# Binary cross-entropy on 8192 x 8192: whole-chunk clips, negations and logarithms, and another order of the last loads and negations

## The chip, the cores and the metric

The kernel runs on one core of one Trainium2 chip. The metric is the device time of one execution in microseconds (us). "The time before" is the median of three executions; beside them one execution was recorded by the hardware profiler, and all rows of "the profile" and "the trace" come from that one.

The engines that this kernel uses are DVE (VectorE), ACT (ScalarE), POOL (GpSimd, here only as an issuer of DMAs) and SP (SyncE, an issuer of DMAs too). A DMA transfer is spread over 16 DMA engines; each engine moves 8 of the 128 rows of a transfer.

## The reference

```python
def reference(pred: np.ndarray, target: np.ndarray) -> np.ndarray:
    eps = 1e-7
    pred = np.clip(pred, eps, 1 - eps)
    return -(target * np.log(pred) + (1 - target) * np.log(1 - pred))
```

Both inputs and the output are 8192 x 8192 in fp32. The target holds only zeros and ones, so the value of an element is -log(|p + t - 1|), with p the clipped prediction.

## The kernel before

The 67 million elements are seen as 128 partitions times 524288 columns and cut into chunks, each of which is one contiguous stretch of DRAM with one row for each partition. There are 39 chunks: chunk 0 (the "first" one, 10240 columns), chunks 1 to 35 with `WIDE` = 14336 columns each, and three small ones from `TAIL` (5632, 5632 and 1024 columns; called a, b and c in this document). In the code z is 35, the last wide chunk, and n is 39.

Two buffers hold all data. `ring_p` has three slots of 14336 fp32 columns; chunk k lies in slot k mod 3, is loaded there, is computed in place, and is stored from there. The three small chunks share one slot, side by side. `ring_t` has a single slot of 14336 bf16 columns for the target, so a target can be loaded only when the chunk before has used its own. The DMA turns the target's fp32 into bf16 while it loads.

A chunk passes five instructions, all in place in `ring_p`:

- `clip` (L85, DVE): max with EPS and min with 1 - EPS.
- `merge`, first part (L91, DVE): (t - 1) + p. It is the last reader of `ring_t`.
- `merge`, second part (L94, ACT): the absolute value.
- `merge`, third part (L95, ACT): the logarithm.
- `negate` (L99, DVE): times -1.

Each is applied to the two halves of a chunk one after the other (`halves`), except for the small chunks, where it is applied to the whole.

The order of the work is written out by hand: `tc.manual_schedule()` keeps the instructions of each engine in the order of the program, and the framework adds the waits between engines. So an instruction that waits holds up all that stands behind it on its engine.

The queues: pred of chunk 0 is loaded on ACT's queue; all other loads (L70 for pred, L73 for target) are issued by GpSimd. Stores (L79) are issued by GpSimd as well up to chunk z - 1; from chunk z on they are issued by SP. On GpSimd the order in the loop is: target k + 1, store k, pred k + 2. In the last round of the loop (k = z - 1) pred of all three small chunks is issued; their targets come behind the merges of chunk z.

At the end DVE's order is: negation of the first half of z, clips of a, b and c, merge of a, negation of the second half of z (with the store of z behind it), merge of b, negation of a, merge of c, negation of b, negation of c.

Of the kernel before, what the change touches and what calls it, by code (L numbers as in the profile page):

```python
# [1 line left out]

# [4 lines left out]

EPS = 1e-7

WIDE = 14336  # L10
SLOTS = 3
TAIL = (5632, 5632, 1024)
ROWS = (108, 12, 8)


@with_exitstack
def kernel(
    ctx: ExitStack,
    tc: tile.TileContext,
    pred: bass.AP,  # L20
    target: bass.AP,
    out: bass.AP,
):
    nc = tc.nc
    fp32 = mybir.dt.float32
    low = mybir.dt.bfloat16
    Alu = mybir.AluOpType
    Act = mybir.ActivationFunctionType
    P = nc.NUM_PARTITIONS

    R, C = pred.shape
    total = R * C // P
    rest = total - sum(TAIL)
    n = rest // WIDE
    first = rest - n * WIDE
    assert 0 < first <= WIDE and n > 4 and sum(TAIL) <= WIDE
    spots = [(first, 0)]
    spots += [(WIDE, k % SLOTS * WIDE) for k in range(1, n + 1)]
    c = (n + 1) % SLOTS * WIDE
    for w in TAIL:  # L40
        spots.append((w, c))
        c += w
    n = len(spots)
    z = n - 1 - len(TAIL)
    starts = [sum(w for w, _ in spots[:k]) * P for k in range(n)]

    pool = ctx.enter_context(tc.tile_pool(name="rings", bufs=1))
    ring_p = pool.tile([P, SLOTS * WIDE], fp32, name="ring_p", tag="ring_p")
    ring_t = pool.tile([P, WIDE], low, name="ring_t", tag="ring_t")
    warm = pool.tile([1, 8], fp32, name="warm", tag="warm")  # L50

    def chunk(ap, k):
        flat = ap.rearrange("r c -> (r c)")
        w = spots[k][0]
        return flat[starts[k] : starts[k] + w * P].rearrange("(p w) -> p w", p=P)

    def cols(ring, k, part, c):
        w = spots[k][0]
        i, m = part
        return ring[:, c + i * w // m : c + (i + 1) * w // m]  # L60

    def p_of(k, part=(0, 1)):
        return cols(ring_p, k, part, spots[k][1])

    def t_of(k, part=(0, 1)):
        return cols(ring_t, k, part, spots[k][1] % WIDE)

    def load_p(k):
        queue = nc.scalar if k == 0 else nc.gpsimd
        queue.dma_start(out=p_of(k), in_=chunk(pred, k))  # L70

    def load_t(k):
        nc.gpsimd.dma_start(out=t_of(k), in_=chunk(target, k))  # L73

    def store(k):
        queue = nc.sync if k >= z else nc.gpsimd
        r = 0
        for rows in ROWS if k == n - 1 else (P,):
            queue.dma_start(out=chunk(out, k)[r : r + rows, :], in_=p_of(k)[r : r + rows, :])  # L79
            r += rows  # L80
        assert r == P

    def clip(k, *part):
        p = p_of(k, *part)
        nc.vector.tensor_scalar(  # L85
            out=p, in0=p, scalar1=EPS, scalar2=1 - EPS, op0=Alu.max, op1=Alu.min
        )

    def merge(k, *part):
        p, t = p_of(k, *part), t_of(k, *part)  # L90
        nc.vector.scalar_tensor_tensor(  # L91
            out=p, in0=t, scalar=1.0, in1=p, op0=Alu.subtract, op1=Alu.add
        )
        nc.scalar.activation(out=p, in_=p, func=Act.Abs)  # L94
        nc.scalar.activation(out=p, in_=p, func=Act.Ln)  # L95

    def negate(k, *part):
        p = p_of(k, *part)
        nc.vector.tensor_scalar(out=p, in0=p, scalar1=-1.0, scalar2=None, op0=Alu.mult)  # L99

    halves = (0, 2), (1, 2)
    tail = range(z + 1, n)
    with tc.manual_schedule():
        load_p(0)
        load_t(0)
        load_p(1)
        nc.vector.memset(warm, 1.0)  # L107
        nc.scalar.activation(out=warm, in_=warm, func=Act.Ln)  # L108
        for h in halves:
            clip(0, h)  # L110
        for k in range(z):
            for h in halves:
                merge(k, h)
            load_t(k + 1)
            for h in halves:
                negate(k, h)
            for h in halves:
                clip(k + 1, h)
            store(k)
            for j in (k + 2,) if k + 2 <= z else tail if k + 2 == z + 1 else ():  # L120
                load_p(j)
        for h in halves:
            merge(z, h)
        for j in tail:
            load_t(j)
        negate(z, halves[0])
        for j in tail:
            clip(j)
        merge(z + 1)
        negate(z, halves[1])  # L130
        store(z)
        merge(z + 2)
        negate(z + 1)
        store(z + 1)
        merge(z + 3)
        negate(z + 2)
        store(z + 2)
        negate(z + 3)
        store(z + 3)


# [1 line left out]
_INS = ['pred', 'target']  # L143
_OUTS = [((8192, 8192), 'float32')]


# [23 lines left out]
```

## Time and profile before

| | |
|---|---|
| median of three executions | 1877.36 us (1874.84 to 1878.22) |
| the profiled execution: its time | 1875.12 us |
| the profiled execution: its span | 1873.3 us |
| busy: DVE, ACT, POOL | 1118.1 (60%), 901.6 (48%), 282.8 us (15%) |
| read from HBM, written to HBM | 536.87 MB, 268.44 MB |
| wide target, issue to landing (median) | 35.2 us |
| wide pred load, issue to landing (median) | 44.4 us |
| wide store on GpSimd's queue, issue to landing (median) | 31.1 us |

The span runs from the first to the last instruction of the core; the time of the same execution is 1.8 us longer. A row of the timeline gives the start in the span, the duration, the engine, the line of the kernel, the operation, what is written and read with the shape, the number of instructions merged into the row, and in brackets how long the engine was idle before it and whose work ended that. A DMA instruction on POOL is a row of its own: its duration is the time that GpSimd took to issue it, not that of the transfer. The queue q0 (software_dynamic) is GpSimd's, q1 is SP's and q10 is ACT's.

### The profile page before, as it was taken

The page shows a single profiled execution, that of the slowest core. Times are in us where ns is not written, and L with a number is a line of the kernel's source. Part 1 is how long each engine was busy: PE and PEld are TensorE (multiplying, and loading weights), DVE is VectorE, ACT ScalarE, POOL GpSimd, SP SyncE. Part 2 cuts the span into 40 slices and gives each one's busy share as a digit, 9 for nine tenths or more (in the row PEclk, how much of TensorE's full clock was granted, in tenths as well). Part 3 has the DMA queues.
Part 4 walks back from the last instruction along what each step waited for, and adds up shares of the span by engine and source line. Part 5 has one row for each costly group of instructions (what it writes and reads, how often), then busy time and mean ns, then how long its engine had stood idle before and what let it go on. Part 6 is the DMA issues. An engine that isn't in the chain of part 4 may idle for free.

```text
span 1873.3 us, 697 instructions
## 1 busy us (share of the span) xinstructions
DVE 1118.1 (60%) x226; ACT 901.6 (48%) x152; POOL 282.8 (15%) x116
## 2 busy tenths in 40 slices
DVE  3666565555665566666555665556656655566565
ACT  2654444455555544444445555554444444555554
POOL 0111111111110111111111111011111111111010
DMA  9999999999999999999999999999999999999998
GB/s 334 347 358 356 353 354 351 353 355 356 363 374 372 373 370 354 362 358 353 353 355 354 359 364 374 372 372 370 359 359 356 354 354 354 354 362 362 373 359 315
DMA packets 16870, 671.14 MB, mean 358 GB/s; under 512 B 1889, under 2 KB 1889, under 8 KB 2273
## 3 DMA queue, kind: packets, MB, share of 16 engines
q0 software_dynamic: 16128, 652.22, 97.4%
q1 hardware_dynamic: 592, 13.63, 1.7%
q10 hardware_dynamic: 144, 5.24, 0.7%
q14 instruction: 6, 0.04, 0.0%
HBM read 536.87 MB, written 268.44 MB: 430 GB/s over the span
## 4 chain that ended last, share of the span: by engine, by line
DMA 67%; issue 28%; ACT 2%; DVE 2%; POOL 0%; POOLq 0%; DVEq 0%
DMA ring_t<-in_target_dram 65%; DMA ring_p<-in_pred_dram 1%; DVE ring_p L91 1%; ACT ring_p L95 1%; ACT ring_p L94 1%; DVE ring_p L99 0%; DVE ring_p L85 0%; POOL out_dram L79 0%; POOL ring_p L70 0%; DVEq L165 0%; POOLq L73 0%; POOLq L79 0%; DVEq L91 0%
## 5 line engine op out<-in xcount | busy, mean ns | idle before, releaser
L94 ACT ACTIVATE ring_p<-ring_p 128x7168 f32<-128x7168 f32 (+3 forms) x75 | 451.6, 6021 | 950.5 <-DVE ring_p L91 950.5
L91 DVE SCALAR_TENSOR_TENSOR ring_p<-ring_t,ring_p 128x7168 f32<-128x7168 bf16 (+3 forms) x75 | 554.8, 7437 | 237.0 <-DMA ring_t<-in_target_dram 237.0
L99 DVE TENSOR_SCALAR ring_p<-ring_p 128x7168 f32<-128x7168 f32 (+3 forms) x75 | 285.0, 3801 | 472.3 <-ACT ring_p L95 472.3
L95 ACT ACTIVATE ring_p<-ring_p 128x7168 f32<-128x7168 f32 (+3 forms) x75 | 452.1, 6029 | 2.4
L85 DVE TENSOR_SCALAR ring_p<-ring_p 128x7168 f32<-128x7168 f32 (+3 forms) x75 | 281.8, 3799 | 29.1 <-DMA ring_p<-in_pred_dram 29.1
L79 POOL DMA_DIRECT2D out_dram<-ring_p x35 | 126.9, 3625 | 713.7 <-DVE ring_p L99 713.7
L73 POOL DMA_DIRECT2D ring_t<-in_target_dram x39 | 20.7, 531 | 809.7 <-DVE ring_p L91 808.9
L70 POOL DMA_DIRECT2D ring_p<-in_pred_dram x38 | 135.3, 3561 | 0.0
L108 ACT ACT_TABLE_LOAD x1 | 1.3, 1283 | 1.1 <-PEq L154 1.1
L107 DVE MEMSET warm<- 1x8 f32 x1 | 0.1, 65 | 0.8 <-PEq L154 0.8
L108 ACT ACTIVATE warm<-warm 1x8 f32<-1x8 f32 x1 | 0.2, 207 | 0.0
L154 POOL MEMSET const-float32-0.0<- 128x1 f32 x1 | 0.1, 98 | 0.2 <-issue 0.2
L154 POOL MEMSET const-bfloat16-1.0<- 128x1 bf16 x1 | 0.1, 101 | 0.0
L154 POOL MEMSET const-float32-1.0<- 128x1 f32 x1 | 0.1, 98 | 0.0
L154 POOL MEMSET const-uint8-127<- 128x1 uint8 x1 | 0.1, 98 | 0.0
## 6 DMA issues: line engine op xcount, KB each, us to landing
ring_p<-in_pred_dram POOLq DMA_DIRECT2D x35, 7168.0 KB, 44.4
out_dram<-ring_p POOLq DMA_DIRECT2D x34, 7168.0 KB, 31.1
ring_t<-in_target_dram POOLq DMA_DIRECT2D x35, 3584.0 KB, 35.2
out_dram<-ring_p SPq DMA_DIRECT2D x1, 7168.0 KB, 18.4
ring_p<-in_pred_dram POOLq DMA_DIRECT2D x2, 2816.0 KB, 35.6
out_dram<-ring_p SPq DMA_DIRECT2D x2, 2816.0 KB, 14.7
ring_p<-in_pred_dram ACTq DMA_DIRECT2D x1, 5120.0 KB, 25.9
out_dram<-ring_p POOLq DMA_DIRECT2D x1, 5120.0 KB, 18.0
```

Source lines behind the costliest of these rows:

```text
L70: queue.dma_start(out=p_of(k), in_=chunk(pred, k))
L73: nc.gpsimd.dma_start(out=t_of(k), in_=chunk(target, k))
L79: queue.dma_start(out=chunk(out, k)[r : r + rows, :], in_=p_of(k)[r : r + rows, :])
L85: nc.vector.tensor_scalar(out=p, in0=p, scalar1=EPS, scalar2=1 - EPS, op0=Alu.max, op1=Alu.min)
L91: nc.vector.scalar_tensor_tensor(out=p, in0=t, scalar=1.0, in1=p, op0=Alu.subtract, op1=Alu.add)
L94: nc.scalar.activation(out=p, in_=p, func=Act.Abs)
L95: nc.scalar.activation(out=p, in_=p, func=Act.Ln)
L99: nc.vector.tensor_scalar(out=p, in0=p, scalar1=-1.0, scalar2=None, op0=Alu.mult)
L107: nc.vector.memset(warm, 1.0)
L108: nc.scalar.activation(out=warm, in_=warm, func=Act.Ln)
L154: nc = _bacc.Bacc("TRN2", target_bir_lowering=False, num_devices=1)
```

## The change

- The first chunk has 8192 columns and the small ones have 6656, 6656 and 1024.
- The clip of every wide chunk and of the first one is one instruction instead of two.
- The logarithm leaves `merge` and gets a function of its own, `log`. In the loop, for every k but 1, the two halves get DVE's merge and the absolute value, then one logarithm and one negation follow for the whole chunk. For k = 1 and for z both stay in halves.
- In the loop's last round no pred of a small chunk is loaded. Behind the merges of z the loads are issued chunk by chunk: pred a, target a, pred b, target b, pred c, target c.
- At the end DVE's order becomes: negation of the first half of z, clip a, negation of the second half of z (store of z behind it), merge a, clip b, merge b, negation a, clip c, merge c, negation b, negation c.

```diff
-TAIL = (5632, 5632, 1024)
+TAIL = (6656, 6656, 1024)
...
         nc.scalar.activation(out=p, in_=p, func=Act.Abs)
+
+    def log(k, *part):
+        p = p_of(k, *part)
         nc.scalar.activation(out=p, in_=p, func=Act.Ln)
...
-        for h in halves:
-            clip(0, h)
+        clip(0)
         for k in range(z):
             for h in halves:
                 merge(k, h)
+                if k == 1:
+                    log(k, h)
             load_t(k + 1)
-            for h in halves:
-                negate(k, h)
-            for h in halves:
-                clip(k + 1, h)
+            if k == 1:
+                for h in halves:
+                    negate(k, h)
+            else:
+                log(k)
+                negate(k)
+            clip(k + 1)
             store(k)
-            for j in (k + 2,) if k + 2 <= z else tail if k + 2 == z + 1 else ():
-                load_p(j)
+            if k + 2 <= z:
+                load_p(k + 2)
         for h in halves:
             merge(z, h)
-        for j in tail:
+            log(z, h)
+        a, b, c = range(z + 1, n)
+        for j in a, b, c:
+            load_p(j)
             load_t(j)
         negate(z, halves[0])
-        for j in tail:
-            clip(j)
-        merge(z + 1)
+        clip(a)
         negate(z, halves[1])
         store(z)
-        merge(z + 2)
-        negate(z + 1)
-        store(z + 1)
-        merge(z + 3)
-        negate(z + 2)
-        store(z + 2)
-        negate(z + 3)
-        store(z + 3)
+        merge(a)
+        log(a)
+        clip(b)
+        merge(b)
+        log(b)
+        negate(a)
+        store(a)
+        clip(c)
+        merge(c)
+        log(c)
+        negate(b)
+        store(b)
+        negate(c)
+        store(c)
```

More of the change, by code (lines that the diff above doesn't have):

```diff
@@ L101 @@
     halves = (0, 2), (1, 2)
-    tail = range(z + 1, n)
     with tc.manual_schedule():
```

## The prediction

> **What bounds the kernel now.** I read the page first, then the chain of waits, the timeline of one middle chunk, the timelines and windows of the first 110 us and of the last 80 us, and last the packet records behind the DMA rows.
>
> ```profile
> DVE 1118.1 (60%) x226; ACT 901.6 (48%) x152; POOL 282.8 (15%) x116
> ...
> DMA  9999999999999999999999999999999999999998
> ...
> q0 software_dynamic: 16128, 652.22, 97.4%
> ```
>
> No compute engine is near full; the DMA engines are, from first slice to last. So fewer or wider instructions save nothing by themselves. The change can act only where it makes the DMA engines wait, or stop waiting. One middle chunk in the timeline (start, duration):
>
> ```profile
> 1079.43 15.16 DVE L91 SCALAR_TENSOR_TENSOR ring_p<-ring_t,ring_p 128x7168 f32<-128x7168 bf16 x2 [6.89 <-DMA ring_t<-in_target_dram]
> ...
> 1094.89 0.53 POOL L73 DMA_DIRECT2D ring_t<-in_target_dram  x1 [22.23 <-DVE ring_p L91]
> ...
> 1105.58 6.18 ACT L95 ACTIVATE ring_p<-ring_p 128x7168 f32<-128x7168 f32 x1
> 1111.79 3.89 DVE L99 TENSOR_SCALAR ring_p<-ring_p 128x7168 f32<-128x7168 f32 x1 [8.38 <-ACT ring_p L95]
> 1115.59 7.70 DVE L85 TENSOR_SCALAR ring_p<-ring_p 128x7168 f32<-128x7168 f32 x2
> 1115.97 3.63 POOL L79 DMA_DIRECT2D out_dram<-ring_p  x1 [20.56 <-DVE ring_p L99]
> 1119.59 3.82 POOL L70 DMA_DIRECT2D ring_p<-in_pred_dram  x1
> 1130.11 15.16 DVE L91 SCALAR_TENSOR_TENSOR ring_p<-ring_t,ring_p 128x7168 f32<-128x7168 bf16 x2 [6.82 <-DMA ring_t<-in_target_dram]
> ```
>
> Target lands at 1079.36, the next one at 1130.04: a period of 50.7 us, which is three wide transfers of 16.9 us (each DMA engine moves 8 of the 128 rows, 2.11 us a row in the packet records). The ring serves target, store, pred in turn. The store of this chunk is ready when L79 ends, at 1119.60; the target ahead of it keeps the last engine busy until 1129.7. So it comes 10 us early. L79 and L70 take 3.63 and 3.82 us where L73 takes 0.53: each was issued while a clip ran and ended 0.1 us after that clip half. GpSimd doesn't get a DMA out while DVE runs the clips; L73 at 1797.79, beside a merge, took 0.53.
>
> The end:
>
> ```profile
> 1828.04 6.02 DVE L91 SCALAR_TENSOR_TENSOR ring_p<-ring_t,ring_p 128x5632 f32<-128x5632 bf16 x1 [4.18 <-DMA ring_t<-in_target_dram]
> 1833.98 3.88 DVE L99 TENSOR_SCALAR ring_p<-ring_p 128x7168 f32<-128x7168 f32 x1
> ...
> 1837.89 23.13 SPq L79 DMA_DIRECT2D out_dram<-ring_p  x6
> ```
>
> ```profile
> 1832.00:1838.50 6.50, 6.50 (x3) 4.41 (x1) 0.00 (x0) 1.00 0.10 20
> 1839.00:1871.00 32.00, 12.72 (x5) 16.61 (x5) 0.00 (x0) 1.00 0.93 395
> ```
>
> The window's last columns are DMA share and GB/s. The last loads end at 1835.6 on the slowest engine, the wide chunk's store starts at 1838.8: 3.2 us of idle DMA, because its second negation stands behind the merge of the first small chunk. From there all stores run back to back to the end.
>
> **The change, part by part.** The sum goes against the profiled execution: span 1873.3, time 1875.12.
>
> *Middle chunks (k = 2 to 34).* From the groups by form: ACT 6.18 us for 7168 columns, 4.47 for 5120, so 0.834 ns a column and 12.15 for 14336. DVE tensor_scalar 3.89 and 2.83, so 0.52 ns a column and 7.60 whole. Merge and both Abs stay in halves; the second Abs starts when the second merge ends (1094.6), ends 1100.8; the whole logarithm ends 1112.97 (now 1111.76); the whole negation 1120.6 (now 1115.7); the whole clip 1128.1 (now 1123.3). L79 is issued at 1120.9, inside the clip, and I take it to be held to the clip's end plus 0.12: 1128.2, 48.9 us after the landing (now 40.2). L70 then goes out at once, 0.53. The clip is done 1.9 us before the next target lands, so no merge waits. The store is ready 8.6 us later, covered by the target transfer still in flight, as long as that lasts. When the ring had run empty in the start phase, L79 ended at 62.29 and its first packet ran at 62.85, 0.57 later, with rows at full speed. 1128.2 + 0.57 = 1128.8, against 1129.7 on the slowest DMA engine. Faster engines would wait some us, but they run up to 4.6 us ahead now and no landing depends on them. So the cover holds by 0.9 us: I cost the loop at 0. Bounds: below nothing no, since the slowest engine is already never idle; above, the row around 107 us, where a store's L79 ended 3.5 to 4 us before the target was through and the target's last row took 3.1 instead of 2.13: 0.95 a chunk, 33 chunks, 31 us. I take 0, because the row at 62 is the nearer (there L79 ended 0.4 us ahead on the slowest engine and the last row stayed 2.13), and keep both.
>
> The Trainium skill (DMA: Bandwidth & Descriptors, section Anatomy of one DMA) gives some 2.0 us of fixed time per DMA, setup and completion, where the rows here show 0.57 + 0.33 = 0.9. By the skill's figure two chunks would take an estimated 48.9 + 50.7 + 2.0, so 50.8 us each, and the loop 2 us more; no trace here shows 2.0.
>
> *Start.* 8192 columns for 10240 take 3 x 2048/14336 x 16.9 = 7.2 us of transfers from the front and put them into the small chunks. Pred and target of chunk 0 alternate row by row, 16 rows of 1.22 instead of 1.53, so pred lands at 22.1 (now 26.65); clip 4.4, to 26.5; merges to 35.2; L73 goes out at 35.5, before pred 1 is through (40), where now it comes as the ring runs dry (43.3; 1 to 1.5 us lost). Second Abs to 38.8, logarithm 7.0 to 45.9, negation to 50.3, then the whole clip of chunk 1 to 57.8 holds store 0: data from 58.5, while target 1 ended at 57.0: 1.5 us idle. Store 0 9.8 us, pred 2 16.9, target 2 17.0: lands at 102.8, now 111.4. 8.6 earlier, of which 7.2 is only moved: a gain of 1.4 (0.5 to 2.5). Logarithms and negations in halves for k = 1 keep store 1 ready at 101.7, in time.
>
> *Tail.* T0 is the landing of the last wide target, 1789.8 now. Small rows of 6656 columns take 0.985 us (5632: 0.833), 7.9 a transfer. After: store z-1 to T0+16.6, pred a to 24.5, target a to 32.4 (its issue waits for a half merge only, T0+8). ACT ends its two halves at T0+32.4 as now. DVE clips a to 28.5, negates the second half to 36.3: store z starts at T0+37.3 (SP's issue to data took 0.9), where now it starts at T0+49.0. That is what the move of the negation buys. But by then only pred a and target a are in, and pred b, target b, pred c and target c are still queued, where now nothing is. Two queues share an engine row by row:
>
> ```profile
> ring_p<-in_pred_dram ACTq DMA_DIRECT2D x1, 5120.0 KB, 25.9
> ...
> out_dram<-ring_p SPq DMA_DIRECT2D x1, 7168.0 KB, 18.4
> ```
>
> 5120 KB beside the other queue took longer than 7168 KB alone. So from T0+37.3 each load row of 0.985 waits for a store row of 2.12: pred b has 3 rows left, and ends at 46.6; target b has 5 of 8 rows in when store z is through (T0+62.1) and ends at 65.1; pred c and target c at 67.8. DVE's queue is in written order: the merge of b waits for target b, and behind it stands the negation of a, whose logarithm was done at T0+54.9. Merge b 65.5 to 72.5, negation a to 76.1, store a from 77.0 to 84.9. All else has been moved by 67.8: 9.2 us idle. Logarithm b ends 84.1, negation b 87.8, store b from 88.7: 3.8 us idle, to 96.6; store c to 97.9, and 2.7 us from there to the end, as now. T0+100.6, now T0+83.5.
>
> *Sum.* T0 comes 8.6 earlier, the tail is 17.1 longer: **+8.5**, span 1881.8, time 1883.6. The median of the runs before, 1877.36, lies 2.2 above the profiled execution; on it the forecast is 1877.4 + 8.5 = **1886**.
>
> **Rivals.**
> 1. *Loads are served first (faster).* If store z on SP's queue did not slow the loads on GpSimd's, target b would land at T0+48.4, merge b end at 55.5, store a be ready at 60, store b at 71.6, and all stores would run back to back behind store z, to T0+87.5: 87.5 - 83.5 - 8.6 = -4.6, 1873. It decides at target b landing before T0+56. For it: the two queues that shared rows at the start were ACT's and GpSimd's, not SP's. Against: 25.9 us for 5120 KB. Chance 0.12.
> 2. *The late store starves the ring in every chunk (much slower).* The 0.9 us cover is a sum of five durations; if the event at 107 us is the rule, 0.95 x 33 = 31 us more, 1917; a part of it, 1894 to 1905. Against: nothing of the kind at 62. Chance 0.25.
> 3. *Nothing to see.* If an engine took two load rows to each store row, the 11 load rows would be through at T0+59.8, merge b at 67.2, store a ready at 71.6, and 5.4 of the 9.2 us idle would not be: +3, 1880. For it, nothing; against, the start's rows alternated one for one. Chance 0.08.
> That instructions stay split in the changed kernel I leave out: each is one call.
>
> **How the numbers follow.** My case has 0.55, its own range 1881 to 1891 (start 0.5 to 2.5, tail 4 either way). A measurement of this kernel can tell about 0.2%, 3.8 us, from no change. Faster: rival 1's most, 0.10. Same: rival 3 and the rest of rival 1, 0.09. Slower: my case, rival 2, 0.81. The range leaves out half of rival 1 and the upper third of rival 2: 1873 to 1908.
>
> **What would show it.** Right: L79 in the loop near 7.3 us and L70 near 0.5; target landings still 50.7 apart; target 2 landing near 103; the small b target landing some 65 us after the last wide one; a window of nearly no DMA of about 9 us before store a and one of about 4 before store b. Wrong: landings 51 to 52 apart with a dip in DMA share at each store (rival 2); the b target within 50 us and no gap ahead of store a (rival 1); or L79 at 0.5 us inside the clip, which would refute the held issue.

## The result, and the profile after

The changed kernel takes 1896.7 us (median of five executions, 1893.4 to 1897.6) against 1878.2 for the kernel before (five executions). The ratio estimated from all of them is 1.0088, 95% interval 1.0071 to 1.0105. The forecast was slower, 1886 against 1877.4; the sign was right, the size about half of what came. The profiled execution has a span of 1895.7 us (1873.3 before), its time is 1897.6. The comparison of the steps below is between these two spans: +22.4 us.

The same lines of the page:

```profile
DVE 1110.3 (59%) x156; ACT 898.5 (47%) x118; POOL 298.2 (16%) x116
...
DMA  9999999999999999999999999999999999999996
...
q0 software_dynamic: 16128, 652.22, 96.9%
```

DVE has 70 instructions fewer and ACT 34, and together they are busy 11 us less. Nothing of that is seen in the time: the DMA engines are full as before, but for the last slice. One middle chunk in the timeline:

```profile
1076.62 15.16 DVE L91 SCALAR_TENSOR_TENSOR ring_p<-ring_t,ring_p 128x7168 f32<-128x7168 bf16 x2 [2.04 <-DMA ring_t<-in_target_dram]
...
1098.02 12.15 ACT L98 ACTIVATE ring_p<-ring_p 128x14336 f32<-128x14336 f32 x1
1110.20 7.63 DVE L102 TENSOR_SCALAR ring_p<-ring_p 128x14336 f32<-128x14336 f32 x1 [18.42 <-ACT ring_p L98]
1117.74 7.62 DVE L85 TENSOR_SCALAR ring_p<-ring_p 128x14336 f32<-128x14336 f32 x1
1118.12 7.36 POOL L79 DMA_DIRECT2D out_dram<-ring_p  x1 [25.52 <-DVE ring_p L102]
1125.47 0.53 POOL L70 DMA_DIRECT2D ring_p<-in_pred_dram  x1
1127.75 15.16 DVE L91 SCALAR_TENSOR_TENSOR ring_p<-ring_t,ring_p 128x7168 f32<-128x7168 bf16 x2 [2.39 <-DMA ring_t<-in_target_dram]
```

Each duration is the one worked out ahead (12.15, 7.60, 7.60, 7.3, 0.5) to 0.1 us, and the store's issue ends 48.9 us after the target's landing (1125.48 - 1076.6), as forecast. But the next merge starts 51.13 us after the last one, not 50.7. The end:

```profile
1860.57 7.09 DVE L91 SCALAR_TENSOR_TENSOR ring_p<-ring_t,ring_p 128x6656 f32<-128x6656 bf16 x1 [17.34 <-DMA ring_t<-in_target_dram]
1867.58 3.62 DVE L102 TENSOR_SCALAR ring_p<-ring_p 128x6656 f32<-128x6656 f32 x1
...
1871.22 15.05 SPq L79 DMA_DIRECT2D out_dram<-ring_p  x5
```

```profile
1829.63 56.65 SPq L79 DMA_DIRECT2D out_dram<-ring_p  x6
```

```profile
1842.00:1861.00 19.00, 1.66 (x2) 6.14 (x2) 0.00 (x0) 1.00 0.99 344
1862.00:1872.00 10.00, 9.96 (x4) 4.30 (x1) 0.00 (x0) 1.00 0.00 1
1872.50:1880.00 7.50, 1.30 (x2) 7.47 (x3) 0.00 (x0) 1.00 0.93 398
1880.00:1883.50 3.50, 3.49 (x2) 1.23 (x2) 0.00 (x0) 1.00 0.00 0
```

The single row is SP's: store z is issued at 1829.63, when pred b is half in and target b still to come. DVE waits 17.3 us for target b, and the negation of a, whose logarithm is done, stands behind that wait. DMA stands still for 10 us ahead of store a and for 3.5 ahead of store b. Ahead of these gaps, in the packet records, a row of target b (1.00 us) and a row of store z (2.13 us) follow each other in turn on each DMA engine, from 1838.4 to 1857.1.

Where the 22.4 us come from can be read from the starts of two merges, of chunk 2 and of the last wide chunk, before and after:

```profile
111.49 15.16 DVE L91 SCALAR_TENSOR_TENSOR ring_p<-ring_t,ring_p 128x7168 f32<-128x7168 bf16 x2 [1.76 <-DMA ring_t<-in_target_dram]
...
1789.86 15.16 DVE L91 SCALAR_TENSOR_TENSOR ring_p<-ring_t,ring_p 128x7168 f32<-128x7168 bf16 x2 [6.87 <-DMA ring_t<-in_target_dram]
```

```profile
102.24 15.16 DVE L91 SCALAR_TENSOR_TENSOR ring_p<-ring_t,ring_p 128x7168 f32<-128x7168 bf16 x2 [1.76 <-DMA ring_t<-in_target_dram]
...
1793.36 15.16 DVE L91 SCALAR_TENSOR_TENSOR ring_p<-ring_t,ring_p 128x7168 f32<-128x7168 bf16 x2 [2.24 <-DMA ring_t<-in_target_dram]
```

The loop's 33 chunks take 51.246 us each instead of 50.860, +12.7; the end takes 102.4 instead of 83.5, +18.9; chunk 2 starts 9.2 earlier. Of the last two, 7.2 us are transfers that were only moved from the front to the end.

### The profile page after: what moved, and what is told of

The parts are those of the page before. It is cut to its first block, busy times and chain, and to the rows that moved or that the text cites. A ratio compares the mean times of both kernels' runs of the same rounds, so it can differ in the third digit from the quotient of the medians.

```text
span 1895.7 us, 554 instructions
## 1 busy us (share of the span) xinstructions
DVE 1110.3 (59%) x156; ACT 898.5 (47%) x118; POOL 298.2 (16%) x116
## 4 chain that ended last, share of the span: by engine, by line
DMA 68%; issue 27%; DVE 3%; another core or an unknown queue 1%; ACT 1%; POOLq 0%; DVEq 0%; POOL 0%
DMA ring_t<-in_target_dram 65%; DMA ring_p<-in_pred_dram 3%; DVE ring_p L91 2%; DVE ring_p L85 0%; ACT ring_p L94 0%; ACT ring_p L98 0%; DVE ring_p L102 0%; DVEq L178 0%; POOLq L73 0%; POOL ring_t L73 0%; POOLq L79 0%; DVEq L91 0%
## 5 line engine op out<-in xcount | busy, mean ns | idle before, releaser
L94 ACT ACTIVATE ring_p<-ring_p 128x7168 f32<-128x7168 f32 (+3 forms) x75 | 452.1, 6028 | 980.3 <-DVE ring_p L91 980.3
L102 DVE TENSOR_SCALAR ring_p<-ring_p 128x14336 f32<-128x14336 f32 (+4 forms) x41 | 279.5, 6820 | 646.5 <-ACT ring_p L98 646.5
L98 ACT ACTIVATE ring_p<-ring_p 128x14336 f32<-128x14336 f32 (+4 forms) x41 | 445.2, 10859 | 1.3
L79 POOL DMA_DIRECT2D out_dram<-ring_p x35 | 257.6, 7359 | 877.4 <-DVE ring_p L102 877.4
L85 DVE TENSOR_SCALAR ring_p<-ring_p 128x14336 f32<-128x14336 f32 (+3 forms) x39 | 279.1, 7156 | 23.9 <-DMA ring_p<-in_pred_dram 23.9
L70 POOL DMA_DIRECT2D ring_p<-in_pred_dram x38 | 20.1, 528 | 0.0
## 6 DMA issues: line engine op xcount, KB each, us to landing
ring_p<-in_pred_dram POOLq DMA_DIRECT2D x35, 7168.0 KB, 36.4
```

What stands on the lines that cost most here:

```text
L85: nc.vector.tensor_scalar(out=p, in0=p, scalar1=EPS, scalar2=1 - EPS, op0=Alu.max, op1=Alu.min)
```

## The experiments

All changes are against the changed kernel unless it says otherwise. "A chunk" is (start of the last wide merge - start of merge 2) / 33 of the profiled execution, "the end" the rest of its span. "Lead" is the time from the end of the store's issue (L79) to the start of the next merge, thus about to the landing of the target in flight; its median over the chunks is 10.6 us in the kernel before and 2.3 in the changed one. Ratios compare with executions of the kernel before that ran beside the experiment.

**The old order at the end.**

```diff
-            if k + 2 <= z:
-                load_p(k + 2)
+            for j in (k + 2,) if k + 2 <= z else tail if k + 2 == z + 1 else ():
+                load_p(j)
...
+        for j in tail:
             load_t(j)
         negate(z, halves[0])
+        for j in tail:
+            clip(j)
+        merge(a)
+        log(a)
         negate(z, halves[1])
         store(z)
...
```

> The changed kernel with the old order at the end: pred of a, b and c issued in the loop's last round, their targets behind the merges of z, the negation of the second half of z behind the merge of a; sizes, start and loop stay changed. Theory 'store z takes rows from the loads' (mine for the tail): here store z starts only when the loads are through, so from the last wide landing to the end it takes some 90 us (target a in at 41.8, merge to 48.9, negation to 52.8, store z 53.7 to 70.6, then a, b, c back to back to 87.7, and 2.7) where the changed kernel took 102.4: the span falls by 12, to about 1884. Rival 'the tail is longer because the small chunks are larger': the larger rows cost the same in either order, and the span falls by less than 4. The loop stays at 51.2 us a chunk under both.

Measured: the end takes 91.1 us, span 1878.9, 1.0006 times the kernel before (0.9995 to 1.0018). The loop, the same code, took 51.08 (51.25 in the changed kernel's own profile). The larger small chunks alone thus lengthen the end by little more than what was moved there: the 83.5 of before and 7.2 us of transfers make 90.7.

**Store z behind the loads.**

```diff
-        queue = nc.sync if k >= z else nc.gpsimd
+        queue = nc.sync if k > z else nc.gpsimd
```

> The changed kernel with one edit: store z is issued on GpSimd's queue, behind the loads of a, b and c, not on SP's. Theory 'store z takes rows from the loads': in one queue it waits until they are through, target b lands 48 us after the last wide target instead of 66.8, store a and b are ready in time, and from that landing to the end it takes 87.5 us instead of 102.4: the span falls by 15, to about 1881. Rival 'the order of DVE alone makes the gap' (the negation of a behind the merge of b): the gap ahead of store a stays at 9 us or so, whatever queue store z is on, and the span falls by less than 4.

The end takes 89.8 us, 12.6 less; span 1880.3; 1.0004 (0.9994 to 1.0013). The rows of its timeline:

```profile
1827.03 0.54 POOL L79 DMA_DIRECT2D out_dram<-ring_p  x1 [19.50 <-DVE ring_p L102]
...
1840.01 7.09 DVE L91 SCALAR_TENSOR_TENSOR ring_p<-ring_t,ring_p 128x6656 f32<-128x6656 bf16 x1 [2.74 <-DMA ring_t<-in_target_dram]
1847.02 3.62 DVE L102 TENSOR_SCALAR ring_p<-ring_p 128x6656 f32<-128x6656 f32 x1
```

The last wide merge started at 1790.49, so merge b starts 49.5 us behind it; in the changed kernel it was 67.2 (1860.57 - 1793.36). DVE's order is the same, and its wait for target b falls from 17.3 to 2.7 us. So DVE's order alone doesn't make the gap: store z, started early on a second queue that shares the DMA engines with the loads, does. The loop, the same code again, took 51.16.

**Clips in halves, and logarithms and negations in halves.** Two kernels, each takes back one part of the whole-chunk work.

```diff
-        clip(0)
+        for h in halves:
+            clip(0, h)
...
-            clip(k + 1)
+            for h in halves:
+                clip(k + 1, h)
```

> The changed kernel with the clips of the first and the wide chunks in halves again; logarithms and negations stay whole. The store's issue (L79) then ends 4.8 us ahead of the end of the target in flight instead of 1.2, pred's issue (L70) stays as late as in the changed kernel. Theory A (the store's issue comes too late for the ring): the loss at each store's end goes, the loop falls from 51.25 to 50.85 us a chunk and the span by 13. Theory B (pred's issue comes too late, just as the store starts): the loss stays, the loop at 51.2. Theory D (the row around 107 us in the kernel before is the rule: a store's issue 4 us ahead with pred's issue 0.5 us ahead costs 0.9 us at the target's last row): the loop at 51.3 to 51.8, the span the same or up to 18 longer.

```diff
-                if k == 1:
-                    log(k, h)
+                log(k, h)
...
-            if k == 1:
-                for h in halves:
-                    negate(k, h)
-            else:
-                log(k)
-                negate(k)
+            for h in halves:
+                negate(k, h)
```

> The changed kernel with logarithms and negations in halves for every wide chunk, clips whole: L79 ends 43.9 us after the target's landing instead of 48.9, L70 0.5 us behind it, so both come 6 us ahead of the target's end. Theories A (late store) and B (late pred): no loss at the store's end, 50.85 us a chunk, the span 13 shorter. Theory C (the two issues 0.5 us apart are what costs, not their lateness): still 51.2.

Neither brought the loop back to 50.85: 51.20 us a chunk with a lead of 6.1 us (1.0092, 1.0069 to 1.0116), and 51.17 with 7.2 (1.0062, 1.0044 to 1.0081). Theory A, as I had put it, fails in both. B comes out in the first and fails in the second, C the other way round, and the 51.3 of D isn't reached. So none of them fits both. The second kernel in the timeline:

```profile
1108.93 7.36 POOL L79 DMA_DIRECT2D out_dram<-ring_p  x1 [20.56 <-DVE ring_p L102]
1116.28 0.53 POOL L70 DMA_DIRECT2D ring_p<-in_pred_dram  x1
1123.30 15.16 DVE L91 SCALAR_TENSOR_TENSOR ring_p<-ring_t,ring_p 128x7168 f32<-128x7168 bf16 x2 [7.12 <-DMA ring_t<-in_target_dram]
```

Its pred is issued 6.5 us ahead of the next merge, as good as in the kernel before (6.7), and the loss is there all the same: a late pred is not needed for it.

**A dose: one us later, one us earlier.**

```diff
+    def again(k):
+        p = p_of(k)[:, 0:1024]
+        nc.scalar.activation(out=p, in_=p, func=Act.Abs)
...
             else:
+                again(k)
                 log(k)
```

> The changed kernel with one more ACT instruction a chunk: the absolute value of the first 1024 columns is taken once more ahead of the whole logarithm (1.04 us; it changes no value). Logarithm, negation, clip and with them the store's issue come 1.0 us later in every middle chunk, nothing else moves. In the runs so far an engine whose target ends less than about one row (2.1 us) behind the store's issue loses at the store's end: 0.25 us at 1 to 2 us, 0.8 below 1. Theory A (lateness costs): covers fall from 1.2 to 1.7 us to 0.2 to 0.7, the loop rises from 51.25 to some 51.7 us a chunk, the span by 10 to 20. Rival (hiccups of the DMA engines that come by chance, alike in all these kernels): the loop stays within 51.1 to 51.3.

```diff
-                if k == 1:
-                    log(k, h)
+                log(k, h)
...
             else:
-                log(k)
                 negate(k)
```

> The changed kernel with logarithms in halves for every chunk, negations and clips whole: the store's issue comes 1.2 us earlier in every middle chunk, covers 2.4 to 2.9 us instead of 1.2 to 1.7. Theory A with a bound of one row (2.1 us): the loss at the store's end goes at first; then engines that have lost nothing run ahead until theirs is below one row, which costs the slowest engine nothing: 50.85 to 51.0 us a chunk, the span 8 to 13 shorter. Rival (hiccups by chance): 51.1 to 51.3.

Later: 51.44 a chunk, span 1903.4, 1.0137 (1.0123 to 1.0152): longer, as theory A has it, but by less than it has (51.7), and outside the rival's range. Earlier: 51.50, span 1903.5, 1.0137 (1.0120 to 1.0154): the opposite of what theory A has. In most of the loop its merges alternate between 50.8 and 52.5 us apart, and this is what the long ones show (the timeline, then one DMA engine's packets; the records don't name the engine, so rows are put together by each starting where the last one ended):

```profile
1118.23 7.36 POOL L79 DMA_DIRECT2D out_dram<-ring_p  x1 [24.28 <-DVE ring_p L102]
1130.45 15.16 DVE L91 SCALAR_TENSOR_TENSOR ring_p<-ring_t,ring_p 128x7168 f32<-128x7168 bf16 x2 [4.98 <-DMA ring_t<-in_target_dram]
```

```
rows of the target on the slowest DMA engine, start + duration in us
... 1119.97+2.13  1122.09+2.13  1124.20+2.13  1126.31+3.74
```

The store's issue ended at 1125.59, pred's at 1126.11; the row that started 0.2 us later took 1.6 us longer than those before it. In the changed kernel the time goes elsewhere, to the last row of the store, on all engines at once. One engine's rows, with the store's issue 1.2 us ahead of the first of them, and the same transfer before:

```
changed  1075.80+2.13 1077.92+2.12 ... 1088.49+2.12 1090.60+2.37 | next transfer from 1092.98
before   1074.61+2.13 1076.74+2.12 ... 1087.30+2.12 1089.42+2.12 | next transfer from 1091.53
```

Over all chunks and engines the store's last row is 0.38 us longer in the changed kernel; in the kernel before the mean is 0.00.

**Pred ahead of the store.**

```diff
             load_t(k + 1)
+            if k + 2 <= z:
+                load_p(k + 2)
...
             store(k)
-            if k + 2 <= z:
-                load_p(k + 2)
```

> The changed kernel with pred k + 2 issued ahead of store k instead of behind it, in every round of the loop; clips, logarithms and negations stay whole, the end stays. The ring then holds a wide pred behind the target in flight when the store's issue comes: a cover of 18 us instead of 1.5. Theory A (late store): no loss, 50.75 to 50.9 us a chunk, and at the start no wait ahead of store 0 (1.5 us): span 13 to 18 shorter, 1878 to 1882. Theory C (two issues 0.5 us apart cost, here target and pred): 51.2 stays. Rival (hiccups by chance): 51.1 to 51.3.

51.02 a chunk, span 1886.7, 1.0046 (1.0028 to 1.0063). Better than 51.25, but not the 50.75 to 50.9 that a long cover should give. Slow rows are now at the end of pred, ahead of the store. With pred of a moved ahead of store z - 1 too, and store z behind the loads:

> Pred ahead of the store in the loop, for the first small chunk too, and store z on GpSimd's queue behind the loads: what the experiments point to. If both causes are right, the loop takes 50.75 to 50.9 us a chunk, the end 88 to 91 us from the last wide landing, the start 2 to 3 us less than in the changed kernel: span 1864 to 1869, faster than the kernel before by 0.2 to 0.5%. If only the end's cause is right: 1878 to 1881.

51.00 a chunk, the end 86.0, span 1870.2: 0.9966 times the kernel before (0.9955 to 0.9978). The loop is again not at 50.75 to 50.9.

**The control, and everything in halves.** Four kernels on one chip: the kernel before; all three steps in halves (both diffs above, and the first clip); that with store z behind the loads; and that with pred ahead.

> The kernel before once more, as a control on the chip of the next three: one look. If the loss in the loop is the changed kernel's own, the loop takes 50.8 to 50.95 us a chunk here too (50.86 in the first profile) and the span 1872 to 1877. If it is a chance of the chip or of the run, the loop is anywhere between 50.8 and 51.3.

> The changed kernel with clips, logarithms and negations in halves for all wide chunks, as before; sizes, start and end stay changed. The store's issue comes 10 us ahead of the target's end again on the slowest DMA engine. Theory (the whole-chunk instructions cost the loop its 0.39 us a chunk through the later issue, although no single one taken back did it): 50.8 to 50.95 a chunk, the span some 1883. Rival (hiccups by chance, or the new sizes): 51.1 to 51.3, the span 1891 to 1896.

> As the last, and store z on GpSimd's queue behind the loads. Both causes taken away, the start's gain kept: 50.8 to 50.95 us a chunk, the end 86 to 90 us: span 1866 to 1871, faster than before by 0.1 to 0.4%.

> Pred ahead of the store in the loop, store z on GpSimd's queue, and all three steps in halves. With whole instructions this order took 51.0 us a chunk, where rows at the end of pred were slow after a store's issue in pred's first rows. With halves the store's issue comes 9 us earlier, in the third row of the target. If the place of the issue in the rows in flight is what counts: 50.75 to 50.9, span 1862 to 1867. If the order itself costs: 51.0 again, 1870.

The kernel before: 50.95 a chunk, span 1878.1. All in halves: 50.84, span 1880.3, 1.0018 (1.0004 to 1.0032). So it is the whole-chunk steps that cost the loop its time, and neither the new sizes nor chance; with them gone the sum of the forecast holds (a span of 1873.3 + 8.5 = 1881.8, for a loop without loss). With store z behind the loads: 50.83, the end 87.3, span 1865.9, median time 1867.2: 0.9936 (0.9913 to 0.9959), the fastest of all. Pred ahead with halves: 50.99 a chunk, 0.9963 (0.9950 to 0.9976), a median of 1872.4 us against 1867.2: that order itself costs 5 us.

**Late, but in halves.** Wide instructions and a late issue had always come together. This takes them apart: half-width instructions, a late issue. The diff is against the kernel with everything in halves.

```diff
+    def again(k):
+        p = p_of(k, halves[1])[:, 0:5632]
+        nc.scalar.activation(out=p, in_=p, func=Act.Abs)
...
+                if h == halves[1] and k > 1:
+                    again(k)
                 log(k, h)
```

> The kernel with all three steps in halves (50.84 us a chunk), and one more ACT instruction a chunk from k = 2 on: the absolute value of 5632 columns of the second half is taken once more ahead of that half's logarithm (4.9 us; it changes no value). No instruction is wider than a half; only the second negation, the clips and the two issues behind them come 4.9 us later, as far as with whole logarithms and negations. Theory (the late issue costs, not the width of an instruction): 51.1 to 51.3 us a chunk, as with clips alone in halves (51.20); the span 8 to 14 longer than 1880.3. Rival (wide instructions cost by themselves, as through a longer hold on GpSimd): 50.8 to 50.9, the span within 3 of it.

51.33 us a chunk, span 1897.4, 17 longer than with all in halves, 1.0084 (1.0060 to 1.0109). One chunk here, then one of the kernel with all in halves:

```profile
1117.01 3.63 POOL L79 DMA_DIRECT2D out_dram<-ring_p  x1 [25.48 <-DVE ring_p L106]
...
1127.62 7.63 DVE L91 SCALAR_TENSOR_TENSOR ring_p<-ring_t,ring_p 128x7168 f32<-128x7168 bf16 x1 [3.29 <-DMA ring_t<-in_target_dram]
```

```profile
1105.62 3.63 POOL L79 DMA_DIRECT2D out_dram<-ring_p  x1 [20.56 <-DVE ring_p L102]
...
1119.78 15.16 DVE L91 SCALAR_TENSOR_TENSOR ring_p<-ring_t,ring_p 128x7168 f32<-128x7168 bf16 x2 [6.83 <-DMA ring_t<-in_target_dram]
```

The issue takes 3.63 us in both; the lead is 7.0 us in the one chunk and 10.5 in the other (over the loop the medians are 6.0 and 10.6). No instruction is wider and no issue is held longer, and the loss is back. What else differs is the added ACT instruction itself, but the changed kernel and the two with one part in halves lose without it.

The table has the lead and the chunk, and two more columns from the packet records. "Late engines" is the share of cases (one DMA engine in one chunk) in which the store's issue ended only after that engine had begun its last row of the target. "Longer" is by how much the store's last row exceeds the 2.12 us of the others, as a mean over engines and chunks.

| kernel | lead (median), us | late engines | longer, us | us a chunk |
|---|---|---|---|---|
| before | 10.6 | 0% | 0.00 | 50.86 |
| before, again | 10.7 | 5% | 0.02 | 50.95 |
| all in halves | 10.6 | 0% | 0.01 | 50.84 |
| logarithms and negations in halves | 7.2 | 30% | 0.15 | 51.17 |
| clips in halves | 6.1 | 63% | 0.25 | 51.20 |
| halves, late | 6.0 | 56% | 0.28 | 51.33 |
| one us earlier | 3.3 | 78% | 0.42 | 51.50 |
| changed | 2.3 | 99% | 0.38 | 51.25 |
| one us later | 1.6 | 100% | 0.67 | 51.44 |

The changed loop took 51.25, 51.08 and 51.16 us in three profiles, so differences of 0.1 to 0.2 in the last column are not to be read. The two middle columns say more than the lead does, because the lead counts to the slowest engine while others run some us ahead of it. Taken over twelve profiles with this order of transfers, the store's last row was 0.44 us longer on average in the 3314 late cases, and 0.01 us in the 2996 others. So it is the late issue that costs at the store's end, and what counts there is each engine's own last target row. The long target rows, as in the kernel with the issue one us earlier, don't follow this division.

## Why the prediction was right or wrong

**Right: what bounds the kernel.** 104 instructions fewer on the compute engines gave nothing back, and the kernel with all three steps in halves again is the faster one (1.0018 against 1.0088 times the kernel before); what counted was the DMA engines' time.

**Right: the start.** Chunk 2's target lands in time for a merge at 102.24; forecast was a landing at 102.8. The gain there is 9.2 - 7.2 = 2.0 us, 1.4 forecast, inside its bounds. That it fits so well is in part luck: pred of chunk 0 landed at 20.4 us, not 22.1, and most of this was lost again on the way, some 0.5 to 1.1 us of it in the last row of store 0 (1.7 to 2.3 us instead of 1.22).

**Right: the end, mechanism and size.** Forecast +17.1 us, measured +18.9. Target b was to land 65 us after the last wide one and merge b to start then; it started 67.2 us after that merge. The gaps were to be 9.2 and 3.8 us and are 10 and 3.5. One term was short: the first rows of store z ran 41 us after the last wide landing, not 37.3, though SP issued it at 36.4. Rival 1 (loads served first) is refuted by target b, which landed at 67 us and not before 56, and by the rows that alternate. The kernel with one queue, where the loads do come first, shows its price: -12.6 us at the end, against the -13.1 that lay between my case and the rival.

**Wrong: the loop at nothing.** The step that failed is "the cover holds by 0.9 us: I cost the loop at 0". The arithmetic of the store's issue was right, to 0.1 us, and the ring hardly runs empty: the store's first row mostly starts when the target's last one ends. But a late issue costs without an empty ring, in longer rows. The term measured +0.386 us a chunk, +12.7 us, by the two profiles. Timed executions agree: kernels that differ only in whole steps or halves are 0.70% apart (1.0088 and 1.0018) with store z on SP's queue and 0.68% (1.0004 and 0.9936) with it on GpSimd's, some 13 us each. This term and the 1.8 us of the end, less 0.6 at the start, are what the forecast of +8.5 lacks of the +22.4. Rival 2 had it as "a part of 0.95 a chunk" at 0.25, with 1894 to 1905 for it, and the time, 1896.7, lies there; its picture of a starved ring is not what the rows show.

I had both rows, 62 us and 107 us, and took the nearer by lead, because the target's last row there stayed at 2.13 and the store's first rows ran at full speed. What the prediction doesn't mention is how that store ended. Its rows on one engine:

```
before, store 0   62.87+1.54 64.40+1.53 ... 72.10+1.52 73.60+2.34 | next transfer from 75.93
```

On all 16 engines the last row took 2.03 to 2.64 us instead of 1.52, a median of 0.78 longer: the only store of the kernel before that was issued as late as all are in the changed one had the loss, at its other end, and with half-width instructions throughout. At 0.78 us a chunk, 33 chunks would have been an estimated 26 us, with the measured 12.7 between that and my 0. The row at 107 us, "a store's issue 3.5 to 4 us ahead, last row 3.1 instead of 2.13", was no exception either: the kernel with the issue one us earlier has a row of that kind, on the slowest engine, in every second chunk. Nothing in the kernel before showed a wide loop with a lead under 10 us and no loss, and more should have gone to rival 2.

The Trainium skill's figure (DMA: Bandwidth & Descriptors, section Anatomy of one DMA), 2.0 us of fixed time, would have made the loop 3 us longer, an estimate (50.8 instead of 50.7 us over 33 chunks; the prediction's "2 us" is a slip). Measured were 12.7, and the 0.57 us from an issue's end to its first row on an idle ring is all that the rows of GpSimd's queue show of such a fixed time ahead of the data.

**What stays open.** Shown is that the late issue of the store costs, by the kernel with halves and a late issue, and not the width of the instructions; and at the store's end, engine by engine, when. Why the store's last row is longer, though it starts some 16 us after the issue, was not settled. Nor was why the target's last row sometimes takes 1 to 1.6 us more when the store's issue has ended shortly before it: this second loss makes the chunk's time not monotone in the lead. Pred ahead still lost some 0.16 us a chunk, though its transfers stand in the queue long before, so the lead to the transfer in flight isn't all of it.

## What to carry to other kernels

Where the DMA queues are full, as here, merging instructions buys nothing by the busy time it saves; ask instead which transfer's issue it moves, and by how much it still leads the end of the transfer in flight, on the fastest DMA engine as well as on the slowest. Here a lead cut from 10.6 to some 7 us or less cost 0.3 to 1.3% of every chunk, though the ring was hardly ever empty. And when a precedent in the trace is to show that something costs nothing, read its transfer to the last row. A store moved to an earlier time on a second queue takes time from the loads that are still due (target b landed 67 us after the last wide target, and merge b started at 49.5 with one queue): put it behind them in their own queue if the last work waits for those loads.

## What the hardware showed that was not expected

- A row can take longer with no gap ahead of it and no second queue beside it. The last row of a store took 0.44 us more on average where the store's issue had ended only after that engine had begun the last row of the transfer in flight, and 0.01 us more elsewhere; a target's row that started 0.2 us after two issues had ended took 3.74 us instead of 2.13.
- The 16 DMA engines don't stay together: in the kernel before, the slowest ends a target 4.4 us behind the fastest in the middle of the run, and every landing is the slowest one's. In the changed kernel, at 1076 us, all end within 0.4 us of each other.
- One whole-width clip holds up one issue on GpSimd for 7.36 us, two half-width ones hold up two for 3.63 and 3.82; an issue gets out in the gap between two clips.
